# The third and fourth column chunk of each down projection computed as a pair with seven products in some blocks, in a two-block transformer kernel

## The chip, the core and the metric

The kernel runs on one core of one Trainium2 chip. The metric is the device time of one execution in microseconds (us), the median of several. Engines are named as in the profile: PE is TensorE's matmuls and PEld its weight loads, DVE is VectorE, ACT is ScalarE, POOL is GpSimd, SP issues the DMAs.

## The reference

256 tokens of width 2048 pass through two transformer blocks, all in fp32. What matters here are the two feed-forward layers and the norm between them:

```
D_MODEL, SEQ, D_FF, D_FF_2 = 2048, 256, 5632, 8192
# end of the first block
z = rmsnorm(h, norm_ffn_g)
h = h + (silu(z @ w_ffn_gate) * (z @ w_ffn_up)) @ w_ffn_down      # 2048 -> 5632 -> 2048
x = rmsnorm(h, norm_final_g)
# second block: starts with a norm and the projection of its result
hn = rmsnorm_2(x, g_mix)
proj = hn @ w_in_2
...                                                                # attention, cross attention
# end of the second block
hm = rmsnorm_2(x, g_mlp)
x = x + square(relu(hm @ w_up)) @ w_down                          # 2048 -> 8192 -> 2048
out = rmsnorm_2(x, g_final)
```

## The kernel before

**Products.** Each fp32 operand is split into a high and a low part, and one product of a 128x128 token block with 128x512 weights is three matmuls of 512 columns: high with high, high with low, low with high (`three`). The activations stay on the chip transposed, as high and low pages (`Act`); weights are loaded from memory once each.

**Units.** The whole program is a list `prog` of units, each with 256 rows by 512 columns of weights (`KG` = 2 blocks of 128 rows) and 12 matmuls as a rule. `emit` walks it: before unit i it emits the split of unit i+4 (ACT copies the high part `whi`, line 455; DVE subtracts it to give the low part `wlo`, line 457), then unit i's matmuls, then what `sched` has put behind that unit, then what `later(lag, ...)` has put `lag` units on. An entry F (an evacuation) stands between two units. There are five buffers for split weights, so the split of unit i+5 waits until PE is through with unit i. Each engine works through its instructions in the order in which they are emitted.

**Plain chunks.** `dense` computes 512 output columns for both token halves (two PSUM banks, taken in turn by `new_acc`: banks 0 and 1, then 2 and 3), and the other four banks rotate for transposes (`bank`).

**Pairs.** `dense2` computes two chunks (2 x 512 columns) at once. Over two blocks of rows, two token halves and two chunks make eight products; a block pair of kind S does them with seven, from sums of activations (`Sums`, made by `sums_of` and `make_sums` on DVE and ACT) and sums of weights (`wu`, `wv`, made in `split` on DVE). It comes as four units: x (6 matmuls), u (6), v (6), y (3), 21 in place of 24. A kind C block has the eight products and two units of 12, and also needs a sum of activations. A pair holds seven banks, and one (bank 7) is left for transposes. After the last S block `early` takes four sums out of PSUM, at the end `finish` takes the rest and calls the evacuation.

**Feed-forward layers.** The first runs in three parts of 4, 4 and 3 chunks of the inner width, the second in four parts of 4. Each part computes its inner chunks (as pairs in the first layer, gate with up; as pairs in the second but for the first two chunks), transposes them into `ffT` (`ff_tr`), and then multiplies by its rows of the down matrix: four `dense` chunks of 512 columns, each added to the residual pages `h`. Behind the last part of the first layer `res_h2` adds the chunk to `h`, squares it on ACT, multiplies by a gain row `gf`, squares it again and, two and three units later, transposes it into `u2T` for the next projection (`to_act` with a gain: two transposes into a bank, then ACT `u2Th` and DVE `u2Tl` read it, and the same again with the next bank). Tables for a rotary embedding (`rope_table`) are made on DVE at units counted back from the end of that layer.

**The tail.** The last chunk (`last_chunk`) computes token half 0, keeping its first weights, then half 1. Its low parts alternate between DVE and POOL; POOL also multiplies finished chunks of `h` by the last gain (`last_gain`).

Of the kernel before, what the change touches and what calls it, by code (L numbers as in the profile page):

```python
# [53 lines left out]
class Sums:  # L54

    def __init__(self, kinds, new):
        self.kinds, self.pages, self.at, last = kinds, [], [], None  # L60
        for i, kind in enumerate(kinds):
            if kind == "S":
                t = new(f"sum{i}")
                self.pages.append(t)
                self.at.append((t, 0, 4))
            elif last is None:
# [13 lines left out]
class Acc:  # L80
# [5 lines left out]
    def __getitem__(self, key):  # L86
        return self.tiles[key[1]][(key[0], *(key[2:] or (slice(None),)))]


# [16 lines left out]
def kernel(  # L106
# [108 lines left out]
    def new_acc():  # L215
        if len(rot) == 1:
            rot[:], pair[0] = [4, 5, 6, 7], 0
        b = 2 * pair[0]
        pair[0] = 1 - pair[0]
        return Acc([psum.tile([P, 512], F32, tag=f"b{b + i}", name="acc") for i in range(2)])  # L220

    def new_seven():
        rot[:] = [7]
        at = {1: 0, 6: 1, 3: 6, 5: 4, 7: 5, 4: 2, 2: 3}
        return {i: psum.tile([P, 512], F32, tag=f"b{b}", name="acc") for i, b in at.items()}
# [70 lines left out]

    def dense2(Wa, ca, Wb, cb, kts, act, sums, kinds, evac):

# [4 lines left out]


        n, hold, last_s = kts // 2, {}, max(i for i, k in enumerate(kinds) if k == "S")
        assert kinds[0] == "S" and kinds[n - 1] == "C"

        def blk(W, c, k, m=1):
            return W[k * P : (k + m) * P, c : c + 512].rearrange("(k p) f -> p k f", p=P)

# [7 lines left out]
        def begin():  # L318
            hold["g"], hold["seen"] = new_seven(), set()

        for p in range(n):
# [10 lines left out]
            if kinds[p] == "S":  # L332
# [9 lines left out]
                def mu(hi, lo, sm_=sm_, fin=fin):  # L342
                    three(5, sm_(0), (hi[:, 0], lo[:, 0]))
                    three(7, sm_(2), (hi[:, 1], lo[:, 1]), fin)
# [14 lines left out]
            else:  # L359
                end = p == n - 1  # L360

                def ma(hi, lo, q=q, sm_=sm_, end=end):
                    for i in range(2):
                        three(5, q(1, i), (hi[:, i], lo[:, i]), end and i == 1)
                    for i in range(2):
                        three(3, sm_(i), (hi[:, i], lo[:, i]), end and i == 1)

# [9 lines left out]
        def early(g):  # L377

            c = [half("c0", [P, 2, 512]), half("c1", [P, 2, 512])]
            nc.scalar.activation(out=c[0][:, 1], in_=g[1], func=AF.Copy)  # L380
            nc.vector.tensor_tensor(out=c[0][:, 0], in0=c[0][:, 1], in1=g[6], op=ALU.add)
            nc.vector.tensor_tensor(out=c[1][:, 1], in0=c[0][:, 0], in1=g[7], op=ALU.add)
            return c

        def finish():
            g, c = hold["g"], hold["c"]
            add = lambda out, a, i: nc.vector.tensor_tensor(out=out, in0=a, in1=g[i], op=ALU.add)  # L387
            add(c[0][:, 0], c[0][:, 0], 5)
            add(c[0][:, 0], c[0][:, 0], 3)
            add(c[1][:, 0], c[1][:, 1], 5)  # L390
            add(c[0][:, 1], c[0][:, 1], 2)
            add(c[1][:, 1], c[1][:, 1], 4)
            evac(c)
# [740 lines left out]
    def evac_down(j):  # L1134
        def fn(acc):
            for t in range(2):
                d = env["h"][t][:, j * 512 : (j + 1) * 512]
                nc.vector.tensor_tensor(out=d, in0=d, in1=acc[:, t], op=ALU.add)
            if j == 3:
                free(env["ffT"])  # L1140
        return fn
# [429 lines left out]
    def wide_sums(p):  # L1571
# [4 lines left out]
        return fn  # L1576

    def evac_wide2(j):

        def fn(c):  # L1580
            if j == 0:
                env["ffT"] = new_act("ffT", 16)
            for t in range(2):
# [133 lines left out]
    for i, (c0, n) in enumerate(parts):  # L1717
# [155 lines left out]
```

## Time and profile before

| | |
|---|---|
| time, median of three runs | 2568.67 us (2565.29 to 2569.63) |
| the profiled execution | 2562.91 us, span from first to last instruction 2561.1 us |
| PE / PEld busy | 2530.6 us (99%) / 2118.6 us (83%) |
| DVE / ACT / POOL busy | 1726.7 (67%) / 1293.0 (50%) / 64.0 us (2%) |
| granted TensorE clock | 0.998 |
| the chain that ended last | PE 95%, DVE 2%, ACT 1%, issue 1% |
| read from memory | 468.55 MB, 184 GB/s over the span |

Busy shares are averages over stages. PE's busy time counts pipelined matmuls whose ends are modelled, so a stall is best read from the starts of two neighbouring matmuls.

### The profile page before, as it was taken

The page shows a single profiled execution, that of the slowest core. Times are in us where ns is not written, and L with a number is a line of the kernel's source. Part 1 is how long each engine was busy: PE and PEld are TensorE (multiplying, and loading weights), DVE is VectorE, ACT ScalarE, POOL GpSimd, SP SyncE. Part 2 cuts the span into 40 slices and gives each one's busy share as a digit, 9 for nine tenths or more (in the row PEclk, how much of TensorE's full clock was granted, in tenths as well). Part 3 has the DMA queues.
Part 4 walks back from the last instruction along what each step waited for, and adds up shares of the span by engine and source line. Part 5 has one row for each costly group of instructions (what it writes and reads, how often), then busy time and mean ns, then how long its engine had stood idle before and what let it go on. Part 6 is the DMA issues. An engine that isn't in the chain of part 4 may idle for free.

```text
span 2561.1 us, 32697 instructions
## 1 busy us (share of the span) xinstructions
PE 2530.6 (99%) x12302; PEld 2118.6 (83%) x12302; DVE 1726.7 (67%) x2083; ACT 1293.0 (50%) x1712; POOL 64.0 (2%) x69
## 2 busy tenths in 40 slices
PE   9999999999999999999999999999999999999998
PEld 7888788888888888888889878889878878878787
DVE  5755565556996689668865658565686685775774
ACT  5445344445554455445554445464554454463553
POOL 1000000000000000000000000000100000000002
PEclk9999999999999999999999999999999999999999
DMA  7565566655666566666646735564656565656563
GB/s 256 159 165 177 152 196 189 190 181 188 203 200 205 186 194 201 205 203 193 210 157 184 193 110 166 180 191 121 200 157 208 180 202 189 188 189 192 182 213 129
DMA packets 261278, 472.82 MB, mean 185 GB/s; under 512 B 21130, under 2 KB 50576, under 8 KB 260864
## 3 DMA queue, kind: packets, MB, share of 16 engines
q1 hardware_dynamic: 258544, 461.77, 57.4%
q0 software_dynamic: 2544, 8.96, 1.1%
q8 instruction: 96, 1.57, 0.3%
q14 instruction: 62, 0.51, 0.1%
q10 hardware_dynamic: 32, 0.01, 0.0%
HBM read 468.55 MB, written 2.12 MB: 184 GB/s over the span
## 4 chain that ended last, share of the span: by engine, by line
PE 95%; DVE 2%; ACT 1%; issue 1%; DMA 0%; SPq 0%; POOL 0%; ACTq 0%; POOLq 0%; DVEq 0%
PE acc L272 60%; PE acc L316 28%; PE pt L506 1%; DVE wlo L457 1%; ACT whi L455 1%; PE pt L512 1%; PE ptr L730 1%; PE acc L1627 0%; PE po L750 0%; PE sc L1310 0%; DMA raw<-in_w_in_dram 0%; PE ptT L554 0%; PE sc L1309 0%; PE psi L1380 0%; DVE c L387 0%
## 5 line engine op out<-in xcount | busy, mean ns | idle before, releaser
L457 DVE TENSOR_TENSOR wlo<-raw,whi 128x1024 fp32r<-128x1024 f32 (+5 forms) x889 | 1025.9, 1165 | 589.0 <-ACT whi L455 577.7
L455 ACT ACTIVATE whi<-raw 128x1024 fp32r<-128x1024 f32 (+5 forms) x896 | 888.8, 1005 | 634.9 <-PE acc L272 488.1
L272 PE MATMUL acc<-whi,ffTh 128*128 128x512 f32 x864 | 333.9, 392 | 0.0
L272 PE MATMUL acc<-wlo,ffTh 128*128 128x512 f32 x832 | 323.8, 389 | 0.0
L272 PE MATMUL acc<-whi,ffTl 128*128 128x512 f32 x800 | 311.7, 390 | 0.0
L316 PE MATMUL acc<-whi,sum 128*128 128x512 f32 x792 | 268.7, 390 | 0.0
L272 PE MATMUL acc<-whi,uTh 128*128 128x512 f32 (+2 forms) x512 | 199.4, 389 | 1.1 <-ACT whi L455 1.1
L272 PE MATMUL acc<-whi,uTl 128*128 128x512 f32 (+2 forms) x512 | 194.3, 379 | 0.5 <-DVE uTl L498 0.5
L272 PE MATMUL acc<-wlo,uTh 128*128 128x512 f32 (+2 forms) x512 | 194.2, 379 | 0.0
L272 PEld LDWEIGHTS acc<-whi,ffTh 128*128 128x128 f32 x864 | 162.2, 188 | 32.8
L272 PEld LDWEIGHTS acc<-wlo,ffTh 128*128 128x128 f32 x832 | 156.3, 188 | 31.7
L272 PEld LDWEIGHTS acc<-whi,ffTl 128*128 128x128 f32 x800 | 150.2, 188 | 31.5
L316 PEld LDWEIGHTS acc<-whi,sum 128*128 128x128 f32 x792 | 148.7, 188 | 30.9
L316 PE MATMUL acc<-whi,zTh 128*128 128x512 f32 x429 | 168.5, 393 | 0.0
L316 PE MATMUL acc<-wlo,zTh 128*128 128x512 f32 x429 | 167.1, 389 | 0.6 <-DVE wlo L457 0.6
L316 PE MATMUL acc<-whi,zTl 128*128 128x512 f32 x429 | 167.1, 390 | 0.0
L316 PE MATMUL acc<-wlo,sum 128*128 128x512 f32 x396 | 154.1, 389 | 0.0
L272 PE MATMUL acc<-whi,u2Th 128*128 128x512 f32 (+2 forms) x352 | 132.6, 377 | 0.0
L272 PE MATMUL acc<-whi,u2Tl 128*128 128x512 f32 (+2 forms) x352 | 129.0, 366 | 0.0
L272 PE MATMUL acc<-wlo,u2Th 128*128 128x512 f32 (+2 forms) x352 | 128.8, 366 | 0.0
L272 PEld LDWEIGHTS acc<-whi,uTh 128*128 128x128 f32 x512 | 96.8, 189 | 22.6 <-issue 5.2
L316 PE MATMUL acc<-whi,x4Th 128*128 128x512 f32 x273 | 107.6, 394 | 5.9 <-ACT whi L455 5.9
(540 smaller groups left out, 4149.9 us busy)
## 6 DMA issues: line engine op xcount, KB each, us to landing
raw<-in_w_in_dram SPq DMA_DIRECT2D x167, 512.0 KB, 3.8
raw<-in_w_down_dram SPq DMA_DIRECT2D x128, 512.0 KB, 4.8
raw<-in_w_ffn_down_dram SPq DMA_DIRECT2D x88, 512.0 KB, 3.8
raw<-in_w_up_dram SPq DMA_DIRECT2D x86, 512.0 KB, 3.8
raw<-in_w_out_dram SPq DMA_DIRECT2D x64, 512.0 KB, 4.2
raw<-in_w_ffn_gate_dram SPq DMA_DIRECT2D x55, 512.0 KB, 3.7
raw<-in_w_ffn_up_dram SPq DMA_DIRECT2D x55, 512.0 KB, 4.6
raw<-in_w_up_dram SPq DMA_DIRECT2D x84, 256.0 KB, 3.2
```

The source lines that it names most:

```text
L272: nc.tensor.matmul(dst, lhsT=v if tr else u, rhs=u if tr else v, start=st, stop=end and j == 2, skip_group_check=True,)
L316: nc.tensor.matmul(g, lhsT=u, rhs=v, start=st and j == 0, stop=stop and j == 2, skip_group_check=True)
L455: nc.scalar.activation(out=hv, in_=r, func=AF.Copy)
L457: eng.tensor_tensor(out=l[:, : u.kn, : u.cn], in0=r, in1=hv.bitcast(F32), op=ALU.subtract)
L506: nc.tensor.transpose(pt[:, a, t * P : (t + 1) * P], src(t, k + a), ident)
L512: nc.tensor.transpose(pt[:, t * P : (t + 1) * P], src(t, k + a), ident)
L730: nc.tensor.transpose(pt[:, j], s[:, j, c * P : (c + 1) * P], ident)
```

## The change

1. In each part of both feed-forward layers two of the four down chunks become a pair (chunks 2 and 3; in the last part of the second layer chunks 0 and 1, after chunk 2 alone). In the first layer's third part the kinds are "SCCSCC", with seven banks. In all other parts a new kind D is used, "SDDDSDDD" and, in the last part, "SDDSDSDD": D is the eight products without a sum, which needs an eighth bank, so no bank is left for transposes while such a pair runs. `early` then takes out two more sums and `finish` one fewer. There are 15 S blocks more in all.
2. The sums of `ffT` that S and C blocks need are made by `ff_sums`, from unit 7 (3 in the last part) of the part's down stage on, one each 1.5 units.
3. Evacuations: `evac_down2` adds both chunks of a pair at once; `evac_each` calls the old one for each chunk in turn.
4. The sums for the second layer's first part (`wide_sums`) are spread over units 4 to 14, before units 3 to 10.
5. In `evac_wide2` the four ACT passes (Relu and Square for each token half) are put behind later units, and the first transposes come one unit later for pair 0.

```
     def new_acc():
-        if len(rot) == 1:
+        if len(rot) < 4:
             rot[:], pair[0] = [4, 5, 6, 7], 0
...
-    def new_seven():
-        rot[:] = [7]
-        at = {1: 0, 6: 1, 3: 6, 5: 4, 7: 5, 4: 2, 2: 3}
+    def new_sums(eight):
+        rot[:] = [] if eight else [7]
+        at = {1: 0, 6: 6, 5: 4, 7: 5, 8: 1, 3: 7, 2: 2, 4: 3} if eight else {1: 0, 6: 1, 3: 6, 5: 4, 7: 5, 4: 2, 2: 3}
...
-                        three(5, q(1, i), (hi[:, i], lo[:, i]), end and i == 1)
+                        three(8 if eight else 5, q(1, i), (hi[:, i], lo[:, i]), end and i == 1)
                     for i in range(2):
-                        three(3, sm_(i), (hi[:, i], lo[:, i]), end and i == 1)
+                        three(3, q(0, i) if eight else sm_(i), (hi[:, i], lo[:, i]), end and i == 1)
...
+    def ff_sums(u, kinds, gap=1.5):
...
+        for i, p in enumerate(p for p, k in enumerate(kinds) if k != "D"):
+            sched(u + gap * i, (0, fn(p)))
+
+    def evac_down2(j):
+        def fn(c):
+            for t in range(2):
+                d = env["h"][t][:, j * 512 : (j + 2) * 512]
+                nc.vector.tensor_tensor(out=d, in0=d, in1=c[t].rearrange("p a f -> p (a f)"), op=ALU.add)
+            free(*c)
+            free(env["ffT"], env["ffTs"])
+        return fn
+
+    def evac_each(j, evac, done):
+        def fn(c):
+            for i in range(2):
+                evac(j + i)(View(c, i))
+            free(*c)
+            done()
+        return fn
...
+            lag, gap = (6, 2) if j == 0 else (3, 1)
             for t in range(2):
-                nc.scalar.activation(out=c[t], in_=c[t], func=AF.Relu, scale=env["r"][:, t : t + 1])
-                nc.scalar.activation(out=c[t], in_=c[t], func=AF.Square)
-            lag, gap = (5, 2) if j == 0 else (3, 1)
+                later((2 if j == 0 else 1) * (t + 1), act(t))
...
-        for j in range(4):
+        kinds = "SDDDSDDD" if i < 2 else "SCCSCC"
+        ff_sums(U() + 7, kinds)
+        for j in range(2):
             dense(w_ffn_down[0], 512 * j, 512, 4 * n, A("ffT"), full, k_off=4 * c0, evac=res_h2(j) if i == 2 else evac_down(j))
+        dense2(
+            w_ffn_down[0], 1024, w_ffn_down[0], 1536, 4 * n, A("ffT"), A("ffTs"), kinds,
+            evac_each(2, res_h2, lambda: free(env["ffTs"])) if i == 2 else evac_down2(2), k_off=4 * c0)
...
-                sched(U(), (3, wide_sums(0)), *[(1, wide_sums(p)) for p in range(1, 8)])
+                sched(U(), (4, wide_sums(0)), *[(1.5, wide_sums(p)) for p in range(1, 8)])
...
-        for j in range(4 if i < 3 else 3):
+        kinds_d = "SDDDSDDD" if i < 3 else "SDDSDSDD"
+        ff_sums(U() + (7 if i < 3 else 3), kinds_d)
+        for j in range(2) if i < 3 else (2,):
             dense(w_down_2[0], 512 * j, 512, 16, A("ffT"), full, k_off=16 * i, evac=evac_last(j) if i == 3 else evac_down(j))
+        o = 1024 if i < 3 else 0
+        dense2(
+            w_down_2[0], o, w_down_2[0], o + 512, 16, A("ffT"), A("ffTs"), kinds_d,
+            evac_each(0, evac_last, lambda: free(env["ffTs"])) if i == 3 else evac_down2(2), k_off=16 * i)
```

The first place is the first layer's third part, where down chunk 1 ends and chunk 2 (now the pair) begins. On DVE there stood, before, the residual's four passes for a chunk (lines 1144 and 1148), two splits, and `u2Tl` for its transposes:

```order
L457 TENSOR_TENSOR wlo<-raw,whi 128x1024 x3
L1144 TENSOR_TENSOR h_4597<-h_4597,acc 128x512
L1148 TENSOR_TENSOR h_4597<-h_4597,gf 128x512
L1144 TENSOR_TENSOR h_4598<-h_4598,acc 128x512
L1148 TENSOR_TENSOR h_4598<-h_4598,gf 128x512
L457 TENSOR_TENSOR wlo<-raw,whi 128x1024 x2
L498 SCALAR_TENSOR_TENSOR u2Tl_10450<-pt,gains,u2Th_10448 128x256 x2
L457 TENSOR_TENSOR wlo<-raw,whi 128x1024
```

In the changed kernel (line 1165 is the old 1144, 1169 the old 1148, 480 the old 457, 521 the old 498; lines 1206 to 1213 are the rotary table, 553 to 568 and 518 a sum of activations) the same place on DVE reads:

```order
L518 TENSOR_TENSOR sum_10615<-f,sum_10615 128x512
L1165 TENSOR_TENSOR h_4597<-h_4597,acc 128x512
L1169 TENSOR_TENSOR h_4597<-h_4597,gf 128x512
L1165 TENSOR_TENSOR h_4598<-h_4598,acc 128x512
L1169 TENSOR_TENSOR h_4598<-h_4598,gf 128x512
L480 TENSOR_TENSOR wlo<-raw,whi 128x1024
L1206 TENSOR_SCALAR kk<-ang 128x112
...
L480 TENSOR_TENSOR wlo<-raw,whi 128x1024
L553 TENSOR_TENSOR f<-ffTh_9702 128x512
L568 TENSOR_TENSOR f<-f 128x256
L518 TENSOR_TENSOR sum_10616<-f,sum_10616 128x256
L521 SCALAR_TENSOR_TENSOR u2Tl_10560<-pt,gains,u2Th_10558 128x256 x2
```

A sum now stands ahead of the residual's passes, and the table and another sum between them and `u2Tl`. On PE the transposes of that chunk stand, in the changed kernel, inside the pair's first S block, between its units u and v (line 332 is the old 316, a product of a pair; 535 the old 512):

```order
L332 MATMUL acc<-wlo,sum_10613 128x512
L332 MATMUL acc<-whi,sum_10613 128x512
L535 MATMUL pt<-con,h_4597 128x128
L535 MATMUL pt<-con,h_4598 128x128
L535 MATMUL pt<-con,h_4597 128x128
L535 MATMUL pt<-con,h_4598 128x128
L332 MATMUL acc<-whi,sum_10613 128x512
L332 MATMUL acc<-wlo,sum_10613 128x512
```

Before, they stood between two plain units of 12 matmuls, with four banks to rotate in; now both pairs of transposes use bank 7.

The second place is POOL's queue at the tail. Before (line 1616 is the last gain, 457 a low part):

```order
L1616 TENSOR_TENSOR h_4597<-h_4597,gfin 128x512
L1616 TENSOR_TENSOR h_4598<-h_4598,gfin 128x512
L457 TENSOR_TENSOR kept<-raw,kept 128x1024
L457 TENSOR_TENSOR wlo<-raw,whi 128x1024 x3
L1616 TENSOR_TENSOR h_4597<-h_4597,gfin 128x512
L1616 TENSOR_TENSOR h_4598<-h_4598,gfin 128x512
```

In the changed kernel (1671 is the old 1616):

```order
L480 TENSOR_TENSOR kept<-raw,kept 128x1024
L480 TENSOR_TENSOR wlo<-raw,whi 128x1024
L1671 TENSOR_TENSOR h_4597<-h_4597,gfin 128x512
L1671 TENSOR_TENSOR h_4598<-h_4598,gfin 128x512
L1671 TENSOR_TENSOR h_4597<-h_4597,gfin 128x512
L1671 TENSOR_TENSOR h_4598<-h_4598,gfin 128x512
L480 TENSOR_TENSOR wlo<-raw,whi 128x1024 x2
```

The four gain passes for chunks 0 and 1 moved in ahead of the last two low parts that POOL makes.

## Rows read from the trace of the kernel before

**Rows 1.** The page: span and busy time of each engine.
```profile
span 2561.1 us, 32697 instructions
...
PE 2530.6 (99%) x12302; PEld 2118.6 (83%) x12302; DVE 1726.7 (67%) x2083; ACT 1293.0 (50%) x1712; POOL 64.0 (2%) x69
```

**Rows 2.** Waits of PE: total us, times, longest.
```profile
PE acc L316 <- ACT whi L455: 5.9, 3, 2.0
```

**Rows 3.** Timeline at pair 0's end, second layer's second part (start, us, engine).
```profile
2061.02 3.26 DVE L387 TENSOR_TENSOR c<-c,acc 128x512 f32<-128x512 f32 x5
...
2063.80 0.39 PE L316 MATMUL acc<-wlo,sum 128*128 128x512 f32 x1
...
2066.75 0.39 PE L316 MATMUL acc<-whi,x4Tl 128*128 128x512 f32 x1
...
2069.08 2.36 DVE L457 TENSOR_TENSOR wlo<-raw,whi 128x1024 fp32r<-128x1024 f32 x2 [4.80 <-ACT whi L455]
2069.10 0.51 PE L316 MATMUL acc<-whi,x4Th 128*128 128x512 f32 x1 [1.96 <-ACT whi L455]
...
2070.36 0.51 PE L316 MATMUL acc<-wlo,x4Th 128*128 128x512 f32 x1 [0.76 <-DVE wlo L457]
```

**Rows 4.** Timeline of PE where the second layer's first transposes stand.
```profile
1869.14 1.11 PE L506 MATMUL pt<-con,u 128*128 128x128 f32 x4 [5.89 <-DVE u L1565]
```

**Rows 5.** Windows: stretch, its us, PE, PEld, DVE, ACT, POOL, PEclk, DMA share, GB/s.
```profile
1267.40:1336.80 69.40, 69.36 (x321) 57.14 (x320) 49.98 (x75) 38.74 (x66) 0.00 (x0) 1.00 0.52 171
1867.00:1873.80 6.80, 4.66 (x13) 3.89 (x14) 4.92 (x9) 3.35 (x5) 0.00 (x0) 0.50 0.26 77
```

**Rows 6.** Timeline of DVE: a sum of kind S, a split, one of kind C.
```profile
1858.90 0.69 DVE L530 TENSOR_TENSOR f<-x4Th,x4Tl 128x512 f32<-128x512 f32 x1
...
1862.28 1.23 DVE L457 TENSOR_TENSOR wlo<-raw,whi 128x1024 fp32r<-128x1024 f32 x1 [0.26 <-ACT whi L455]
1863.42 0.69 DVE L530 TENSOR_TENSOR f<-x4Th,x4Tl 128x512 f32<-128x512 f32 x1
...
1865.40 0.15 DVE L1089 TENSOR_REDUCE s<-ssx 128x2 f32<-128x8 f32 x1
```

**Rows 7.** Timeline, first layer's third part: evacuation of down chunk 0.
```profile
1284.44 0.68 DVE L1144 TENSOR_TENSOR h<-h,acc 128x512 f32<-128x512 f32 x1
...
1288.05 0.69 DVE L1148 TENSOR_TENSOR h<-h,gf 128x512 f32<-128x512 f32 x1 [0.85 <-ACT junk L559]
...
1290.54 2.36 DVE L457 TENSOR_TENSOR wlo<-raw,whi 128x1024 fp32r<-128x1024 f32 x2 [1.80 <-ACT whi L455]
...
1293.36 0.60 PE L512 MATMUL pt<-con,h 128*128 128x128 f32 x4
```

**Rows 8.** Timeline of DVE: the rotary table and the split behind it.
```profile
1314.88 0.21 DVE L1185 TENSOR_SCALAR kk<-ang 128x112 f32<-128x112 f32 x1
...
1318.40 2.36 DVE L457 TENSOR_TENSOR wlo<-raw,whi 128x1024 fp32r<-128x1024 f32 x2 [1.31 <-ACT whi L455]
```

**Rows 9.** Timeline, second layer's first part: evacuation of chunk 1, inside pair 2.
```profile
1889.71 1.22 DVE L1565 TENSOR_TENSOR u<-u 128x1024 f32<-128x1024 f32 x1
...
1893.85 0.33 PE L506 MATMUL pt<-con,u 128*128 128x128 f32 x1 [0.51 <-DVE ffTl L495]
```

**Rows 10.** Timeline, second layer's last part: third transposes and low parts of `ffT`.
```profile
2477.76 0.60 PE L506 MATMUL pt<-con,c 128*128 128x128 f32 x4
...
2479.03 0.69 DVE L495 TENSOR_TENSOR ffTl<-pt,ffTh 128x512 fp32r<-128x512 f32 x1 [1.02 <-ACT ffTh L494]
```

**Rows 11.** Timeline of the tail: the last chunk's first matmuls and its low parts.
```profile
2530.41 0.62 PE L1627 MATMUL acc<-kept,ffTh 128*128 128x512 f32 x2
...
2534.22 5.79 POOL L457 TENSOR_TENSOR wlo<-raw,whi 128x1024 fp32r<-128x1024 f32 x2 [8.16 <-ACT whi L455]
2535.07 2.68 DVE L457 TENSOR_TENSOR wlo<-raw,whi 128x1024 fp32r<-128x1024 f32 x1 [0.67 <-ACT whi L455]
2539.97 2.53 POOL L1616 TENSOR_TENSOR h<-h,gfin 128x512 f32<-128x512 f32 x2
```

More of the change, by code (lines that the diff above doesn't have):

```diff
@@ L65, in __init__ @@
                 self.at.append((t, 0, 4))
+            elif kind == "D":
+                self.at.append(None)
             elif last is None:
@@ L87, in __getitem__, with __init__ @@
         return self.tiles[key[1]][(key[0], *(key[2:] or (slice(None),)))]
+class View:
+    def __init__(self, c, i):
+        self.c, self.i = c, i
+    def __getitem__(self, key):
+        return self.c[key[1]][:, self.i]
 class Quad:
@@ L295, in dense, with dense2 @@
         return hold
-    def dense2(Wa, ca, Wb, cb, kts, act, sums, kinds, evac):
+    def dense2(Wa, ca, Wb, cb, kts, act, sums, kinds, evac, k_off=0):
+        eight = "D" in kinds
         n, hold, last_s = kts // 2, {}, max(i for i, k in enumerate(kinds) if k == "S")
-        assert kinds[0] == "S" and kinds[n - 1] == "C"
+        assert kinds[0] == "S" and kinds[n - 1] != "S" and not (eight and "C" in kinds)
         def blk(W, c, k, m=1):
+            k += k_off
             return W[k * P : (k + m) * P, c : c + 512].rearrange("(k p) f -> p k f", p=P)
@@ L318, in begin @@
         def begin():
-            hold["g"], hold["seen"] = new_seven(), set()
+            hold["g"], hold["seen"] = new_sums(eight), set()
         for p in range(n):
@@ L342, in mu @@
                 def mu(hi, lo, sm_=sm_, fin=fin):
-                    three(5, sm_(0), (hi[:, 0], lo[:, 0]))
+                    three(5, sm_(0), (hi[:, 0], lo[:, 0]), fin and eight)
                     three(7, sm_(2), (hi[:, 1], lo[:, 1]), fin)
@@ L382, in early @@
             nc.vector.tensor_tensor(out=c[1][:, 1], in0=c[0][:, 0], in1=g[7], op=ALU.add)
+            if eight:
+                for t in range(2):
+                    nc.vector.tensor_tensor(out=c[t][:, 0], in0=c[t][:, t], in1=g[5], op=ALU.add)
             return c
@@ L387, in finish @@
             add = lambda out, a, i: nc.vector.tensor_tensor(out=out, in0=a, in1=g[i], op=ALU.add)
-            add(c[0][:, 0], c[0][:, 0], 5)
-            add(c[0][:, 0], c[0][:, 0], 3)
-            add(c[1][:, 0], c[1][:, 1], 5)
+            if eight:
+                add(c[1][:, 0], c[1][:, 0], 8)
+                add(c[0][:, 0], c[0][:, 0], 3)
+            else:
+                add(c[0][:, 0], c[0][:, 0], 5)
+                add(c[0][:, 0], c[0][:, 0], 3)
+                add(c[1][:, 0], c[1][:, 1], 5)
             add(c[0][:, 1], c[0][:, 1], 2)
@@ L1138, in fn @@
                 nc.vector.tensor_tensor(out=d, in0=d, in1=acc[:, t], op=ALU.add)
-            if j == 3:
-                free(env["ffT"])
         return fn
@@ L1576, in wide_sums, with fn, g @@
         return fn
+    def ff_sums(u, kinds, gap=1.5):
+        def fn(p):
+            def g():
+                if p == 0:
+                    env["ffTs"] = Sums(kinds, lambda nm: half(nm, [P, 8, P], F32R))
+                sums_of(env["ffT"], env["ffTs"], p)
+            return g
+        for i, p in enumerate(p for p, k in enumerate(kinds) if k != "D"):
+            sched(u + gap * i, (0, fn(p)))
+    def evac_down2(j):
+        def fn(c):
+            for t in range(2):
+                d = env["h"][t][:, j * 512 : (j + 2) * 512]
[10 more added lines that the diff above has]
+        return fn
     def evac_wide2(j):
@@ L1582, in fn, with act, g @@
                 env["ffT"] = new_act("ffT", 16)
+            def act(t):
+                def g():
+                    nc.scalar.activation(out=c[t], in_=c[t], func=AF.Relu, scale=env["r"][:, t : t + 1])
+                    nc.scalar.activation(out=c[t], in_=c[t], func=AF.Square)
+                return g
+            lag, gap = (6, 2) if j == 0 else (3, 1)
             for t in range(2):
-                nc.scalar.activation(out=c[t], in_=c[t], func=AF.Relu, scale=env["r"][:, t : t + 1])
-                nc.scalar.activation(out=c[t], in_=c[t], func=AF.Square)
-            lag, gap = (5, 2) if j == 0 else (3, 1)
+                later((2 if j == 0 else 1) * (t + 1), act(t))
             for i in range(2):
```

## Prediction

> **What bounds the kernel now.** The page comes first: PE is busy for 2530.6 of 2561.1 us, DVE for 67% [rows 1]. So the end is set by the number of matmuls and by the moments in which PE stands. From 2063.80 to 2066.75 PE starts 13 matmuls further, 0.227 us each [rows 3]; that is the price of one matmul of 512 columns. PE's waits say where it stands: 5.9 us in three places for ACT's high parts [rows 2]. The timeline of one of them [rows 3] shows how: after a pair's end DVE's five sums take until 2064.3, ACT then does the pair's Relu and Square passes, and only behind them the next split; PE's starts at 2066.75, 2069.10 and 2070.36 should lie 0.227 apart and lie 2.12 and 1.03 us too far apart, 3.15 us together. The other long stand is one of 5.9 us at the second layer's first transposes, which wait for DVE [rows 4]. The windows then show that the granted clock was 0.50, the lower of the two levels, for the 6.8 us from 1867.0, after PE had stood, and 1.00 in the third part of the first layer, where DVE is busy for 50.0 of 69.4 us and PE never stands [rows 5]. That last window matters most: a DVE with 19 us to spare looks free, but it works in order, and its spare time lies in chains in which it waits for ACT.
>
> **What the change removes.** 15 S blocks save 3 matmuls each: 45 x 0.227 = 10.2 us, all on PE's path. ACT's passes leave the place before the next split: 3 x 3.15 = 9.45 us [rows 2, 3]; DVE's sums end 2 us after the pair's end, a split takes 1.13 more, and the S block in front gives PE 21 x 0.227 = 4.8 us, so nothing of the stall should be left. Together 19.6 us.
>
> **What it adds, stage by stage.** Prices on DVE: a low part of 1024 columns 1.13 (two in 2.36, [rows 8]), and I take the same for `wu`; a pass of 512 columns 0.65 (five in 3.26, [rows 3]), so the two `wv` 1.3. A sum of kind S holds DVE for 3.4 us up to the next low part (1858.90 to 1862.28), 3.1 without the wait for that split; one of kind C 2.0 (1863.42 to 1865.40) [rows 6].
>
> *Parts with D (five of seven).* Two sums, two S blocks, and an evacuation by two passes of 1024. Two sums cost 6.8 us at units 7 and 8 against a lead of four units, 4 x 2.72 = 10.9 us: hidden. At the pair's end DVE has four sums and two passes of 1.13; counted from the end of its splits as in [rows 3] it is free 3.7 us after the end and the next low part is there at 4.85, while PE needs it at 4.8 + 0.2: hidden with 0.1 to spare. I take nothing; if that cover fails it costs about 1 us in each of five places. The bytes loaded stay the same; an S block asks for its two tiles at once, as in the pairs of before, and is taken as nothing too (below by nothing, above by 1 us for each part).
>
> *Third part of the first layer.* Here six sums and two S blocks meet `res_h2`. The evacuation of a chunk runs on DVE from 1284.44 to 1288.74, 4.3 us, as each gain pass waits for ACT's square of the same rows, and the next low part comes 1.8 us later still, since ACT squares twice more [rows 7]. The table costs, with ACT's pass and the split behind it, 3.5 us (1314.88 to 1318.40) [rows 8]. Now DVE in the new order, on the clock of before, from the end of the two splits at 1292.8: sum S 3.1, `u2Tl` 0.8, unit x 3.6 (`wu`, low part, `wv`), sum C 2.05, `u2Tl` 0.8, low part of u 1.85 (it waits for ACT), of v 1.15, sum C 2.05, low part of y 0.75, sum S 3.1: 19.3 us, to 1312.1. Only then the evacuation of chunk 1: 1316.4. PE has its transposes at 1293.36 [rows 7], then 0.35 and 36 matmuls (8.15) to 1301.9, unit x 1.36 to 1303.2, and u, which waits for its low part, to 1306.2. Next in its queue stand the transposes of chunk 1, which need the evacuation: PE stands for 10 us. The second two of them use the same bank 7 and wait until DVE has read the first two; in DVE's queue that is behind 1.8 of waiting, a low part 1.13, the table with its split 3.5, a low part 1.13, a sum C 2.05 and `u2Tl` 0.45: 1326.8. So unit v starts at 1327.2 in place of 1304.95: 22 us. The same bank holds the next two transposes behind a low part 1.1, a sum 2.05 and a `u2Tl` 0.5: another 4 us before unit y. After such a stand the clock was at its lower level [rows 5], where starts lie about 0.43 apart; some 6 matmuls of it cost 1 us more. Sum 27 us. From below: if DVE came to the evacuation with nothing queued ahead of it, at 1302, PE would still wait for 4.3 + 1.8 + 1.1 + 3.5 + 1.1 + 2.05 + 0.45 = 14.3 us from there, 12 to 13 over what it does now; I take 27, since the queue is counted from rows.
>
> At this part's end `evac_each` evacuates two chunks in a row, where before one was left. DVE's chains make 8.6 us from about 0.85 after the end; the transposes of both, asked for after two units of the next projection (12 x 0.227 x 416/512 = 2.2 us each, an estimate), start at 9.5 in place of 4.75: 4.7 us. The later four wait for banks behind ACT's two last squares, two splits and four `u2Tl`: 2.3 more. Sum 7; from below 4 (ACT's squares hidden), from above 9.
>
> *Second layer's first part.* Spreading `wide_sums` adds and takes no work. DVE has no pause from 1846.9 on until the second chunk's pass at 1889.71 [rows 9], and all eight sums stand ahead of that pass before and after. So the first stand shrinks from 5.9 to 1.4 us by my count, and what is gained there PE waits for at the second chunk's transposes. The first sum now stands behind one more split, for which DVE waits 0.9 us: I take +1.5 us; from below -5 (if the second wait is shorter and the clock stays up), from above +4.
>
> *Second layer's last part.* The transposes at 2477.76 fill what unit 6 needs at 2481.8 (0.35, a unit of 2.72, 0.35, two matmuls); its low part came at 2479.7 [rows 10]. Now DVE has, from about 2474.5, a sum S 3.1, an `ffTl` 0.65, unit x 3.6, a sum S 3.1 and then this `ffTl` 0.65: 2485.6. PE waits 3.8 us. Then the pair starts on bank 0, which chunk 2 has just used: its evacuation stands behind two low parts, an `ffTl`, the third sum and a short low part, 7.8 us, to 2493.4, where PE comes at 2490.5: 2.9 more. Sum 6.7; from below 2 (only the bank).
>
> *Tail.* POOL took up its last two low parts 3.8 us after the last chunk's start and ended them 9.6 after it, just in time for the units at 1.36 us each [rows 11]. Now four gain passes of 1.27 stand ahead (two in 2.53), the first possible at 2.4; the low parts start at 7.5, 3.7 us later, and PE with them: 3.7 us. A DVE low part beside POOL takes 2.68 in place of 1.2 [rows 11], which is why I take nothing off. The Trainium skill ("SBUF — State Buffer", "SBUF: two separate sides") says more: GpSimd and a VectorE instruction with two SBUF inputs exclude each other for a whole instruction. By that rule the two later residual adds, which now read both inputs from SBUF, could each wait for a gain pass of 1.27, and the term would be up to 6.2. The row shows such a delay only for low parts.
>
> **Sum.** -10.2 - 9.45 + 27 + 7 + 1.5 + 6.7 + 3.7 = +26.3 us. On the profiled execution's 2562.9 that is 2589.2; the median of the runs lies 5.8 us above it, so the forecast is 2595 us, 1.0% slower. About 0.2% (5 us) is what a measurement of this kernel can tell from no change.
>
> **Rivals.** (a) *Half the price.* DVE reaches the third part's places earlier than my count, and the floors hold: 13 + 4 + 4 + 2 + 4 with 19.6 saved, and nothing for `wide_sums`: +7, 2576. For it: the pauses in DVE's chains may overlap more than I add. Against: each step is a measured chain, in order. 0.2. (b) *Not slower.* PE does not stand at chunk 1's transposes and the part's end, because the evacuation gets through while unit u runs: without the 34 us the sum is -8, 2561. It decides as soon as both places together cost less than 7.7 us. For it: 19 us of DVE pause in that part [rows 5] against some 23 us of new work (six sums 14, two S blocks 9). Against: bank 7 alone has delayed PE already where a transpose waited for DVE's read of the one before [rows 9], and here two chains in a row hang on it. 0.1. (c) *The stalls stay.* ACT's passes, put later, delay another split, or five pairs' ends cost 1 us or more: +10 to +15, 2608. For it: 0.1 us to spare at these ends. Against: ACT has four units of lead there. 0.12. (d) *The spread sums pay.* The last 6.5 us of the first part are won: 2588; within the forecast's own range. The forecast itself, 2583 to 2604, has 0.58.
>
> **Chances and range.** The faster cases lie in (b): 0.08; no change, the rest of (b) and the low end of (a): 0.06; slower 0.86. The range takes the forecast, (a) but for its low end and half of (c): 2571 to 2608.
>
> **What would show it.** PE's waits should have lost the three of 2.0 us for ACT, and gained stands of some 10 us each at `pt<-con,h` in the third part (released by DVE's gain pass and by `u2Tl`), with a granted clock near 0.5 behind them; that part, 69.4 us before, should take 93 to 95. 45 matmuls fewer on PE. The pass on `u` for chunk 1 should end no earlier than before. In the last part PE should wait for `ffTl` and for chunk 2's evacuation, at the tail for POOL. The forecast is wrong if PE passes the third part's S block without standing, or if DVE's sums there take much less than 3.4 and 2.0 us.

## The result and the profile after

The changed kernel takes 2594.17 us in the median of four runs (2593.11 to 2594.88), against 2567.86 us (2565.29 to 2569.63) for the kernel before: a ratio of 1.0103, 95% interval 1.0085 to 1.012, so 1.0% slower and 26.3 us. The forecast was 2595 us. Its total is right; two of its terms are well off, and they cancel, as the experiments show.

The page of the changed kernel, to be held against [rows 1]:

```profile
span 2592.9 us, 32979 instructions
...
PE 2533.0 (98%) x12257; PEld 2117.4 (82%) x12257; DVE 1860.2 (72%) x2305; ACT 1329.6 (51%) x1768; POOL 68.4 (3%) x69
```

PE has 45 matmuls fewer and yet a span 31.8 us longer; DVE has 133.5 us more to do. PE's waits (engine, line, what it waited for; total us, times, longest), against [rows 2]:

```profile
PE pt L535 <- DVE h L1169: 14.5, 5, 7.6
PE pt L535 <- DVE u2Tl L521: 12.0, 2, 9.8
PE pt L529 <- DVE u L1586: 7.8, 2, 6.7
PE acc L285 <- ACT ffTh L517: 3.4, 1, 3.4
...
PE acc L1682 <- ACT whi L478: 1.8, 1, 1.8
...
PE acc L1682 <- POOL wlo L480: 1.5, 1, 1.5
PE acc L1682 <- DVE wlo L480: 1.2, 1, 1.2
...
PE acc L332 <- DVE h L1656: 0.8, 1, 0.8
```

The three waits of 2.0 us for ACT are gone. In their place stand the forecast's two of some 10 us at `pt<-con,h` (7.6 and 9.8), one for the third `ffT` of the last part (3.4; ended by ACT's `ffTh`, where the forecast had named DVE's `ffTl`), and three at the tail (line 1682), of which the forecast had only POOL's.

The windows of the changed kernel (stretch, its us, PE, PEld, DVE, ACT, POOL, PEclk, DMA share, GB/s): the first layer's third part, the middle of it, and the tail. The first answers to the first of [rows 5].

```profile
1264.28:1358.22 93.94, 71.84 (x307) 57.62 (x306) 66.60 (x103) 41.39 (x65) 0.00 (x0) 0.85 0.40 128
1299.00:1334.00 35.00, 12.90 (x41) 8.83 (x40) 23.65 (x44) 14.31 (x27) 0.00 (x0) 0.61 0.20 66
2553.11:2592.90 39.79, 26.42 (x97) 20.17 (x95) 14.19 (x22) 10.80 (x20) 16.63 (x10) 0.82 0.16 57
```

The third part takes 93.9 us in place of 69.4, and DVE is busy in it for 66.6 us in place of 50.0. In the 35 us from 1299 PE did 12.9 us of work, and the granted clock fell to 0.61 of full speed in the mean.

The timeline of that place on DVE, ACT and PE (start, us, engine), which answers to [rows 7, 8]:

```profile
1305.45 0.68 DVE L553 TENSOR_TENSOR f<-ffTh,ffTl 128x512 f32<-128x512 f32 x1
...
1307.88 0.69 DVE L518 TENSOR_TENSOR sum<-f,sum 128x512 fp32r<-128x512 f32 x1 [0.69 <-ACT sum L517]
1308.49 0.68 DVE L1165 TENSOR_TENSOR h<-h,acc 128x512 f32<-128x512 f32 x1
...
1310.71 0.47 PE L535 MATMUL pt<-con,h 128*128 128x128 f32 x1 [7.58 <-DVE h L1169]
...
1312.85 0.47 PE L535 MATMUL pt<-con,h 128*128 128x128 f32 x1 [1.67 <-DVE h L1169]
...
1322.63 0.48 DVE L521 SCALAR_TENSOR_TENSOR u2Tl<-pt,gains,u2Th 128x256 fp32r<-128x256 f32 x1
...
1323.17 0.69 PE L535 MATMUL pt<-con,h 128*128 128x128 f32 x2 [9.85 <-DVE u2Tl L521]
```

DVE reaches chunk 1's residual add (line 1165) at 1308.49, straight from a sum; PE's transposes follow at 1310.71 and 1312.85; and the next two wait until `u2Tl` has read bank 7 at 1322.63, behind a split, the rotary table, a split and a sum. The forecast had put the end of the sum at 1312.1, that of the evacuation at 1316.4 and that of `u2Tl` at 1326.8; in the changed kernel this part starts 3.15 us earlier, and they end at 1308.6, 1312.8 and 1323.1, within 0.6 us of it.

Stage by stage, between the starts of the first matmul of one stage and of the next in the two profiled executions (net: with the saved matmuls counted apart):

| stage | before | after | net of matmuls | forecast |
|---|---|---|---|---|
| five parts with D | | -1.34 to -1.36 each | 0.0 | 0 |
| three w_up stages (the two pairs of a part) | 88.2 | 84.87 | -3.3 each | -3.15 each |
| first layer, third part | 69.39 | 93.94 | +25.9 | +27 |
| from there to the second feed-forward layer | 497.51 | 506.65 | +9.1 | +7 |
| second layer's first up stage | 97.44 | 99.20 | +1.75 | +1.5 |
| last part, down stage | 67.22 | 71.60 | +6.4 | +6.7 |
| tail | 30.70 | 39.81 | +9.1 | +3.7 |

Eight transposes have moved from the third part into the stage behind it. With the saved matmuls the stages sum to 32.2 us, and the changed kernel spends 0.4 less ahead of the first of them: together the 31.8 us by which the spans differ. The medians differ by only 26.3; numbers 7 and 8 show why.

### The profile page after: what moved, and what is told of

Same layout as the page of the kernel before. It is cut to its first block, busy times and chain, and to the rows that moved or that the text cites. A ratio compares the mean times of both kernels' runs of the same rounds, so it can differ in the third digit from the quotient of the medians.

```text
span 2592.9 us, 32979 instructions
## 1 busy us (share of the span) xinstructions
PE 2533.0 (98%) x12257; PEld 2117.4 (82%) x12257; DVE 1860.2 (72%) x2305; ACT 1329.6 (51%) x1768; POOL 68.4 (3%) x69
## 4 chain that ended last, share of the span: by engine, by line
PE 92%; DVE 4%; ACT 2%; issue 1%; DMA 0%; POOL 0%; SPq 0%; POOLq 0%; ACTq 0%; DVEq 0%
PE acc L285 47%; PE acc L332 39%; DVE wlo L480 1%; PE pt L529 1%; ACT whi L478 1%; PE pt L535 1%; PE ptr L753 0%; PE po L773 0%; ACT junk L582 0%; PE sc L1331 0%; DVE f L553 0%; PE ptT L577 0%; DMA raw<-in_w_in_dram 0%; PE sc L1330 0%; PE psi L1401 0%
## 5 line engine op out<-in xcount | busy, mean ns | idle before, releaser
L480 DVE TENSOR_TENSOR wlo<-raw,whi 128x1024 fp32r<-128x1024 f32 (+5 forms) x889 | 1015.5, 1156 | 455.4 <-ACT whi L478 440.8
L332 PE MATMUL acc<-whi,sum 128*128 128x512 f32 x928 | 315.2, 391 | 0.1
L332 PEld LDWEIGHTS acc<-whi,sum 128*128 128x128 f32 x928 | 174.8, 188 | 36.7 <-ACT whi L478 0.5
L332 PE MATMUL acc<-wlo,sum 128*128 128x512 f32 x464 | 181.3, 391 | 1.0 <-DVE wlo L480 1.0
L285 PE MATMUL acc<-whi,ffTh 128*128 128x512 f32 x416 | 162.5, 397 | 3.4 <-ACT ffTh L517 3.4
L285 PE MATMUL acc<-wlo,ffTh 128*128 128x512 f32 x400 | 156.4, 391 | 0.0
L285 PE MATMUL acc<-whi,ffTl 128*128 128x512 f32 x384 | 150.4, 392 | 0.0
L332 PE MATMUL acc<-whi,ffTh 128*128 128x512 f32 x361 | 140.2, 392 | 0.8 <-DVE h L1656 0.8
L478 ACT ACTIVATE whi<-wu 128x1024 fp32r<-128x1024 f32 x69 | 73.3, 1062 | 124.6 <-DVE wu L464 93.3
L332 PE MATMUL acc<-wlo,ffTh 128*128 128x512 f32 x349 | 136.6, 391 | 0.0
L332 PE MATMUL acc<-whi,ffTl 128*128 128x512 f32 x337 | 131.8, 391 | 0.0
L478 ACT ACTIVATE whi<-wv 128x1024 fp32r<-128x1024 f32 x69 | 73.3, 1062 | 85.4 <-PE acc L332 39.2
```

Source lines behind the costliest of these rows:

```text
L285: nc.tensor.matmul(dst, lhsT=v if tr else u, rhs=u if tr else v, start=st, stop=end and j == 2, skip_group_check=True,)
L332: nc.tensor.matmul(g, lhsT=u, rhs=v, start=st and j == 0, stop=stop and j == 2, skip_group_check=True)
L478: nc.scalar.activation(out=hv, in_=r, func=AF.Copy)
L480: eng.tensor_tensor(out=l[:, : u.kn, : u.cn], in0=r, in1=hv.bitcast(F32), op=ALU.subtract)
```

## The experiments

All are edits of the changed kernel or of the kernel before, and each ratio is to runs of the kernel before on the same chip. In the code a line `...`, and `...` inside a call, mark what is left out.

**1. Third part in plain chunks.** Its sums are not made either.

```
-        for j in range(2):
+        for j in range(4 if i == 2 else 2):
             dense(w_ffn_down[0], ...)
+        if i == 2:
+            break
```

> The third part of the first layer is four plain chunks again; all else as in the changed kernel. Theory (the two rows of stands at the transposes of chunk 1 and of the pair's end cost what the profile shows): the part goes back from 93.9 to about 69.4 us, the 6.1 us of stands behind it go too, so the time falls by 33 to 35 us, to about 2560 us. Rival (the stands only take up delay that would show elsewhere, since DVE is busier in the later stages as well): it falls by less than 25 us.

Measured: 2559.67 us (2559.23 to 2561.28), ratio 0.9975 (0.9965 to 0.9986), 34.5 us less than the changed kernel. The part is back at 69.4 us and the stage behind it at 497.5. The first theory holds: none of the delay comes up again later.

**2. The sums of the third part early.**

```
-        ff_sums(U() + 7, kinds)
+        ff_sums(U() + (7 if i < 2 else 1), kinds, 1.5 if i < 2 else 1)
```

> The pair of the third part stays, its six sums of activations are made in units 1 to 6 of the part and not in units 7 to 14, so none of them stands ahead of chunk 1's evacuation or of its second read of the bank. Theory (the queue on DVE makes the stand): of the four stands of 7.8, 2.1, 10.3 and 2.5 us the first shrinks to about 3 and the third to about 8; 6 to 9 us less than the changed kernel, about 2587. Rival (one bank for the transposes makes the stand, whatever DVE has queued): the sum of the four stays at 20 us or more and the time within 3 us of the changed kernel.

Measured: 2590.56 us (2588.56 to 2591.14), 3.6 us less. The four stands went from 7.8, 2.1, 10.3 and 2.5 to 0.8, 2.1, 8.3 and 1.5 us. But some 6.8 us of new ones stand earlier, at the last `ffT` and at chunk 0's transposes. So the queue on DVE has a part in these stands, and neither theory had the whole: in both places the sums delayed what stood behind them.

**3. The transposes of chunk 1 later in the pair.**

```
+                if name_T == "u2T" and j == 1:
+                    for a in range(4):
+                        later(5 + a, lambda k=4 * j + a: to_act_one(src, env[name_T], k, gain))
+                    return
```

> The pair of the third part and its sums stay where they are; chunk 1's eight transposes are issued two at a time behind pair units 4 to 7 instead of four at a time behind units 1 and 2. DVE has as much to do as before and there is still only bank 7. Theory (the place of the transposes makes the stands, right behind a late evacuation and two reads of one bank in a row): the four stands of 22.6 us and the lower clock behind them go but for 0 to 4 us, so about 20 us less than the changed kernel, 2572 to 2578. Rival (DVE has too much to do in this part): PE waits for low parts instead, and the time falls by less than 10 us.

Measured: 2592.55 us (2592.11 to 2593.37), 1.6 us less. My theory fell here. PE's waits in this kernel from 1295 to 1345:

```profile
PE pt L542 <- DVE u2Tl L521: 8.3, 1, 8.3
PE acc L332 <- DVE h L1176: 5.9, 2, 5.4
PE acc L332 <- ACT whi L478: 1.6, 1, 1.6
PE acc L332 <- DVE wlo L480: 1.2, 2, 0.8
```

PE still stands inside the first S block, now where the pair needs the banks of chunk 1 (line 1176 is the residual add that reads them), and then for high and low parts; then bank 7's reader stands on DVE behind the second S block's sums of weights. The edit took the place away and left the work on DVE as it was (busy for 66.6 us in both), and the part is only 1.4 us shorter (92.5): the waits are less, but 28 matmuls started some 0.43 us after the one before, as at the lower clock, against 14.

**4. The last part in plain chunks.** Its sums are not made either.

```
-        for j in range(2) if i < 3 else (2,):
+        for j in range(2 if i < 3 else 3):
             dense(w_down_2[0], ...)
+        if i == 3:
+            break
```

> The last part of the second layer is three plain chunks and the last chunk again; all else as in the changed kernel. The prediction's terms (6.7 for the down stage, 3.7 for the tail, less 2.0 for nine matmuls): 8.4 us less, 2586. By the trace of the changed kernel, with the tail 9.3 us longer than before: 13 to 14 us less, about 2580.5.

Measured: 2581.03 us (2579.77 to 2581.32), 13.1 us less: the trace's figure, not the forecast's.

**5. The gain passes at the tail behind the low parts.**

```
-            if j < 2:
-                last_gain(j)
...
-            last_gain(2)
+            for j in range(3):
+                last_gain(j)
```

> POOL's gain passes for chunks 0 and 1 are issued behind all of the last chunk's units, with those of chunk 2, so POOL's last two low parts come straight behind its third. Theory of the prediction (POOL's queue makes the tail's delay): the tail loses 3.7 us or more, 2590 or less. Rival (ACT's high parts wait behind the four squares, and DVE's low parts behind eight sums and adds): the stands of 2.0 and 1.5 us for ACT and DVE stay, only the 1.9 us for POOL goes, so 1 to 2.5 us less, about 2592.

Measured: 2588.87 us (2587.79 to 2590.01), 5.3 less; the tail takes 34.9 us. So POOL's passes cost 4.9 of the 9.1, more than the wait of 1.5 us put down to POOL. By the starts of PE's matmuls, the stand for POOL was 1.9 of it, the stands for ACT and DVE are shorter by 0.7 and 0.4, and the rest is the lower clock, at which 7 matmuls ran in place of 16. The tail of the changed kernel:

```profile
2555.14 3.58 DVE L1656 TENSOR_TENSOR h<-h,c 128x512 f32<-128x512 f32 x4
...
2556.65 6.65 POOL L1671 TENSOR_TENSOR h<-h,gfin 128x512 f32<-128x512 f32 x4 [6.05 <-ACT junk L582]
...
2559.44 3.88 ACT L478 ACTIVATE whi<-raw 128x1024 fp32r<-128x1024 f32 x4
...
2560.53 0.50 PE L1682 MATMUL acc<-whi,ffTh 128*128 128x512 f32 x1 [1.82 <-ACT whi L478]
...
2562.22 0.80 PE L1682 MATMUL acc<-wlo,ffTh 128*128 128x512 f32 x1 [1.18 <-DVE wlo L480]
...
2566.64 0.79 PE L1682 MATMUL acc<-wlo,ffTh 128*128 128x512 f32 x1 [1.50 <-POOL wlo L480]
```

And with the gains behind the low parts:

```profile
2554.77 2.48 DVE L1656 TENSOR_TENSOR h<-h,c 128x512 f32<-128x512 f32 x4
...
2558.38 3.88 ACT L478 ACTIVATE whi<-raw 128x1024 fp32r<-128x1024 f32 x4
...
2560.44 5.81 POOL L480 TENSOR_TENSOR wlo<-raw,whi 128x1024 fp32r<-128x1024 f32 x2 [10.20 <-ACT whi L478]
```

Four residual adds on DVE take 3.58 us beside POOL and 2.48 without it, and the splits on ACT, which stand behind the squares of these adds, start 6.3 us into the tail against 5.6. The page of the Trainium skill that the prediction weighed ("SBUF — State Buffer", "SBUF: two separate sides") says that such an add and a pass of GpSimd exclude each other for a whole instruction. The trace agrees: three adds take 0.68 us each, and the fourth, which starts while a gain pass runs, takes 1.78, 1.1 more.

**6. The last pair's evacuations behind the splits.**

```
     def evac_each(j, evac, done, lag=0):
...
+            done()
+            if lag:
+                later(lag, g)
```

> Both evacuations of the last pair (residual adds, squares, gain passes) are issued four units later, behind all splits of the last chunk; the four sums out of PSUM stay. Theory (the adds and squares ahead of the splits make the tail's delay): all three stands of 5.4 us go, and with them the 20 matmuls at the lower clock, so the tail shrinks from 40.0 to about 31 us and the time by 8 to 9 us, to about 2585.5. Rival (POOL's gains alone): those move behind the low parts here too, so it falls by the same as with the gains moved alone.

Measured: 2586.09 us (2584.11 to 2587.75), 8.1 less, and the tail is back at 30.8 us with no stand in it. The first theory holds: 4.9 us of the tail's delay went with POOL's gains in number 5, and the other 4.1 go with the adds and squares that stood ahead of DVE's and ACT's splits.

**7. The spread of the eight sums alone, on the kernel before.**

```
-                sched(U(), (3, wide_sums(0)), *[(1, wide_sums(p)) for p in range(1, 8)])
+                sched(U(), (4, wide_sums(0)), *[(1.5, wide_sums(p)) for p in range(1, 8)])
```

> The kernel before with only the spread of the eight sums over units 4 to 14. The prediction's term: +1.5 us (the first stand shorter, the second chunk's longer). Rival (the spread pays): -5 us, 2563. By the changed kernel's stage, 99.20 us against 97.44: +1.75.

Measured: 2568.94 us (2564.12 to 2571.88), ratio 1.0002 (0.9993 to 1.0011), which is no difference that the runs can tell. The stage shows it: 99.1 us in place of 97.4, with the first stand down from 6.1 to 1.2 and the second chunk's up from 0.7 to 6.9. The spread does not pay.

This run's profile cleared up something else. This kernel has the three stands for ACT as before; at the first of them, and behind it, its windows read (the columns as above):

```profile
2067.50:2071.50 4.00, 1.29 (x5) 0.52 (x3) 1.27 (x2) 3.97 (x5) 0.00 (x0) 1.00 0.00 0
2071.50:2076.00 4.50, 4.50 (x15) 3.60 (x16) 4.50 (x5) 2.49 (x3) 0.00 (x0) 0.64 0.71 236
```

The same place in the profiled execution of the kernel before:

```profile
2066.50:2070.50 4.00, 1.28 (x5) 0.52 (x4) 1.42 (x2) 3.97 (x5) 0.00 (x0) 1.00 0.00 0
2070.50:2075.00 4.50, 4.50 (x22) 3.72 (x23) 4.50 (x5) 3.00 (x5) 0.00 (x0) 1.00 0.78 253
```

The stand is the same, 3.15 us. Behind it PE does 22 matmuls in 4.5 us in the one and 15 in the other, where the granted clock was at its lower level for some of them. By w_up stage this cost 1.5, 1.5 and 2.6 us more; by the starts of its matmuls 6, 6 and 10 of them ran 0.43 us apart. So the same stand comes at different prices, and the execution of before that was profiled had drawn the lowest one three times.

**8. ScalarE's passes alone, on the kernel before.**

```
-            for t in range(2):
-                nc.scalar.activation(out=c[t], in_=c[t], func=AF.Relu, ...)
-                nc.scalar.activation(out=c[t], in_=c[t], func=AF.Square)
-            lag, gap = (5, 2) if j == 0 else (3, 1)
+            lag, gap = (6, 2) if j == 0 else (3, 1)
+            for t in range(2):
+                later((2 if j == 0 else 1) * (t + 1), act(t))
```

> The kernel before with only ScalarE's four passes put behind later units and the first transposes one unit later. The prediction's term: three stands of 3.15 us go, -9.45, about 2558.5. By the changed kernel's stages 3.3 us each: -10. Rival (the passes delay another split or the transposes): less than 5 us won.

Measured: 2552.6 us (2552.43 to 2553.02), ratio 0.9941 (0.9928 to 0.9953): 14.5 us less than before, where the profiles differ by 10.5, of which the three stages make 9.9. All three stands are gone. The 15 runs of before beside them spread over 5.0 us (2565.14 to 2570.17), these five over 0.6. The mean granted clock of each run is on record, and the time goes with it: among those 15, the run at 0.997 took 2565.14 us, the seven at 0.996 took 2565.36 to 2567.09, and the seven at 0.995 took 2568.19 to 2570.17. The profiled execution of before had 0.998, these five 0.997 to 0.999.

**9. What is left when the third part, the last part and the spread are undone.** The edits of 1 and 4 together, and the old `sched` line of 7.

> The changed kernel with the first layer's third part and the second layer's last part in plain chunks and the eight sums as before: what is left is the pairs of kind D in the five other parts and ScalarE's passes. Theory (terms add up stage by stage): ScalarE's passes alone gave 2552.6; five times six matmuls of 0.227 us are 6.8 us less, 2545.8. Rival (the pairs of kind D cost about 1 us at each end): 2550 or more.

Measured: 2546.58 us (2546.12 to 2546.85), ratio 0.9918 (0.9905 to 0.9932). The terms add up to within 0.8 us. The page:

```profile
span 2544.3 us, 32873 instructions
...
PE 2520.5 (99%) x12272; PEld 2112.4 (83%) x12272; DVE 1811.4 (71%) x2223; ACT 1315.7 (52%) x1747; POOL 66.5 (3%) x69
```

It is the fastest of the study and beats both kernels.

**10. The last part's pair kept and mended.** As 9, with the pair of the last part, its evacuations late as in 6, and its sums apart:

```
-        ff_sums(U() + (7 if i < 3 else 3), kinds_d)
+        ff_sums(U() + (7 if i < 3 else 6), kinds_d, 1.5 if i < 3 else 4)
```

> As the one before, but with the last part's pair kept, its three sums at units 6, 10 and 14 and not 3, 4 and 6, and its evacuations four units later. Theory (the third transposes stand 3.6 us for the sums that ScalarE and DVE do ahead of them, and the tail 9.3 us for the evacuations): both stands and the lower clock behind them go, the last part and tail together take 97.9 - 2.0 = 95.9 to 97 us against 111.4 in the changed kernel, and the time is 1 to 2 us under that with plain chunks, 2544. Rival (the sums only move the stand to a low part or to the pair's first units): the stage stays at 100 us or more, 2548 or more.

Measured: 2547.19 us (2546.95 to 2547.3), ratio 0.992 (0.9907 to 0.9934). The part and the tail take 99.1 us: the stand at the third transposes and the tail's are gone, a stand of 1.8 us is left where the pair takes bank 0 from chunk 2, and one of 0.6 for a low part. With the 2.0 us saved it comes out no better than plain chunks. The theory had the cause of the stands right and the gain too large.

**11 and 12. The third part's pair without transposes in it, with two sums and with six.** Both are number 10 with a pair in the third part, and chunk 1 transposed behind that pair:

```
-                        later(2 + a, lambda k=k: to_act(src, env[name_T], k, gain))
+                        lag = (2, 17, 4, 6)[j] if name_T == "u2T" else 2
+                        later(lag + a, lambda k=k: to_act(src, env[name_T], k, gain))
```

Number 11 has `kinds = "SDDSDD"` there, number 12 has `"SCCSCC"`; nothing else differs.

> As the one before, but the third part of the first layer is a pair too, with kind D in place of C, so two sums in place of six and no bank for transposes while it runs; chunk 1 is transposed behind the pair, chunks 2 and 3 one and three units later than in the changed kernel. Theory (DVE has too much to do in that part: busy for 66.6 us where PE needs 68.0, plus its waits for ScalarE): four sums less take some 8 us off DVE, so the part comes down from 93.9 to 75 us or less, about 2546 to 2550. Rival (the evacuations' chain through ScalarE and the squares costs PE as much with any number of sums): the part stays above 80 us.

Measured: 2569.09 us (2568.46 to 2569.81), ratio 1.0006 (0.9998 to 1.0015). The part takes 76.7 us, between the two theories' bounds, so neither holds as put. The stage behind it takes 14.6 us more than before, and that is why the time is some 20 us over the theory's 2546 to 2550. PE's wait there (1341 to 1420):

```profile
PE acc L285 <- ACT u2Th L520: 8.4, 5, 7.0
```

Chunk 1's transposes now stand in this stage, and ACT makes `u2Th` of them only from 1353.12 on, behind the squares of chunks 2 and 3, while PE's third unit already needs it. That loss is one of place, and no other place was tried. (Chunks 2 and 3 come two and four units later by the edit, not one and three.) Between this kernel and the changed one, place and load differ together; the next one changes the load alone.

> As the kernel with all places mended, which took 2569.1 us and 76.7 us for the first layer's third part, but that part's pair is of kinds SCCSCC again: six sums of activations in place of two is the only difference; no transpose stands in the pair and its one bank is not used. Theory (the load on DVE makes the stands): four sums of about 2.05 us each are 8 us more on DVE, at a place where PE already waits for it, so the part takes 83 to 86 us and the time is 6 to 9 us longer, 2575 to 2578. Rival (the transposes in the pair and their one bank made them, and the sums have room): the part stays at 76 to 79 us, the time within 2 us of 2569.

Measured: 2581.24 us (2580.62 to 2582.54), ratio 1.0054 (1.0037 to 1.0071), 12.2 us more than number 11 (on another chip; by the two ratios 12.3). The windows of the part, first with two sums, then with six:

```profile
1264.45:1341.11 76.66, 70.33 (x299) 55.60 (x298) 59.77 (x90) 38.08 (x57) 0.00 (x0) 0.96 0.44 149
```

```profile
1264.53:1352.05 87.52, 73.90 (x300) 56.72 (x299) 64.69 (x99) 39.61 (x61) 0.00 (x0) 0.92 0.41 137
```

PE's waits in the same stretches, with two sums and with six:

```profile
PE acc L332 <- DVE wlo L480: 2.4, 4, 0.8
PE acc L332 <- DVE h L1166: 2.3, 1, 2.3
PE acc L332 <- ACT whi L478: 1.7, 2, 0.8
```

```profile
PE acc L332 <- DVE h L1166: 6.0, 2, 5.4
PE acc L332 <- DVE wlo L480: 4.2, 7, 0.8
PE acc L332 <- ACT whi L478: 3.4, 2, 1.8
```

Four sums put 4.9 us net on DVE's busy time (C needs fewer adds out of PSUM than D) and 10.9 us on the part. PE's waits are 13.6 us in place of 6.4; of the other 3.7 us the lower clock makes some 2.3, as 18 matmuls in place of 9 started about 0.43 us apart. So with no transpose in the pair and bank 7 unused, the sums make PE stand. They are work for DVE and, one pass each, for ACT; the waits for high parts grew too, and which engine's share is the larger isn't told apart.

## Why the prediction was right, and where two of its terms were wrong

- **45 matmuls, -10.2.** Right: each part with D is shorter by its 1.36 us to within 0.02, so the ends of these pairs, hidden with 0.1 us to spare by the forecast, are hidden (number 9).
- **ScalarE's passes, -9.45.** The mechanism was right, the size was not: 14.5 us by number 8. The term was read off one execution in which the clock had stayed at its upper level behind all three stands. Number 7 shows a stand of the same length with 1.5 to 2.6 us of lower clock behind it. The unprofiled runs of before have the lower mean clock of number 8's list, and their spread goes with the stands. That the lower clock lies behind these three stands in them is inferred; no trace of those runs exists.
- **Third part, +27, and its end, +7.** 34 forecast, 35.0 by stage, and 35.9 by number 1 (34.5 and the 1.36 of six matmuls). The chain was the one described, with the two releasers that were named. Inside the part the split was less good: the four stands make 22.6 us where the forecast had 26, a low part ahead of them makes 1.0, and the lower clock 3.1 (14 matmuls) where it had 1; two of the forecast's times rest on small slips (the parts named add up to 1326.5, not 1326.8, and the splits ended at 1292.9). And the account leaned on bank 7 and the place of the transposes, and number 12 shows that without either PE stands elsewhere, as the sums are too much for this part. By busy time alone DVE's 66.6 us would just fit beside the 68.0 us of matmuls that the part has left; with 26.3 us of waits for ACT they fill it. How many of these waits could be hidden isn't told apart: before, DVE waited 18.7 us for ACT there, and PE never stood. Rival (b) had set 19 us of pause against 23 of new work; busy time rose by 16.6, and the evacuation did not get through all the same.
- **Spread of the sums, +1.5.** Right, 1.65 to 1.75 by stage: the stand moved from the first chunk's transposes to the second's. DVE's work ahead of the second chunk's pass is the same in both orders, and before the change its pauses there were few (the longest 2.1 us, where the forecast said none). By the runs alone it can't be told from nothing.
- **Last part, +6.7.** 6.4 by stage, but with another split. The late third `ffT` took 3.6 us (3.8 forecast), ended by ACT's `ffTh`, which stands behind the sum's pass on ACT. Bank 0 took 1.0: the forecast had 2.9, from 7.8 us of work on DVE of which the items named make only 6.7. And 8 matmuls at the lower clock took 1.7, which were not in the forecast.
- **Tail, +3.7.** This is the term that failed: 9.1 us. The step was "the low parts start at 7.5, 3.7 us later, and PE with them". POOL's low parts start at 10.2, 6.4 later: its first gain pass starts at 3.5 and not at 2.4, and the four take 6.65 us and not 5.1. Yet PE does not follow POOL alone: of the 9.1, POOL's share is 4.9, and the 6.2 us that the prediction gave as the term's upper end is short of it too. What was overlooked is that the evacuation of two chunks puts eight passes on DVE and four squares on ACT ahead of the same splits. 16 matmuls at the lower clock, 3.5 us, are in the 9.1. ACT's splits start 6.3 us into the tail (2559.44 against 2553.11) in place of 1.7 in the kernel before, whose tail starts at 2530.41:

```profile
2532.09 3.89 ACT L455 ACTIVATE whi<-raw 128x1024 fp32r<-128x1024 f32 x4
```

The tail is 5.4 us dearer than forecast and ScalarE's stands gave 5 us more than forecast, so the sum came out. That is luck: from profile to profile the change costs 31.8 us where the terms gave 26.3, and the 5.8 us by which the median of before lay above its profile, which the forecast added, are not there in the changed kernel (its profiled run took 2594.78 us, the median is 2594.17). By the medians: -14.5 and -6.8 for what pays, +34.5, +13.1 and about +1.8 for what does not, make +28.1 against 26.3 measured; where the 1.8 us between them lie is open.

What stays open: whether a pair in the third part can pay with its sums on another engine, or with kind D as in number 11 and chunk 1's transposes at a better place; neither was tried.

## What to carry to other kernels

A saving of matmuls pays where the engine that prepares it has room in that very stage: five parts gave their 1.36 us each, two gave back 35 and 15. Before moving a transpose or a sum out of a stand's way, add up what the preparing engine has to do in the stage, its waits for others included, against the matmuls' time. In the last part the work had room, and putting it elsewhere (number 10) won back 12 of the 15; in the third part it had not, and the stands moved with it. The length of a stand in one profiled execution is not its whole price: if the clock stayed up behind it there, the spread of the runs and their mean clocks tell what the lower clock adds.

## What was unexpected of the hardware

The granted clock behind a stand isn't the same from run to run. After stands of 3.15 us it stayed at 1.00 in the profiled execution of before and fell to the lower level for 6, 6 and 10 matmuls in that of number 7, same instructions, same place. With the stands removed, the spread of the runs on one chip shrank from 5.0 us (15 runs) to 0.6 (five).
